# Block 2's recurrence: outputs as full 128x128 products, state products on column halves, outer products on row halves

## The chip, the cores and the metric

The kernel runs on one core of a Trainium2 chip. The metric is the device time of one execution in microseconds (us). The profile shows one execution of the program, taken on that core by the hardware profiler. TensorE (PE) does the matmuls, VectorE (DVE) and ScalarE (ACT) the elementwise work and the copies out of PSUM, GpSimd (POOL) a few subtractions, and SyncE (SP) issues most weight loads from HBM. In the profile's matmul rows `64*128` is the part of the 128x128 array that the instruction uses (rows*columns), and `64x128` its moving operand.

## What is computed

Two transformer blocks follow each other on 256 tokens of width 1024. The first has band attention, a gated delta rule and a retrieval of experts. The second has a gated linear recurrence (HGRN2), stick-breaking attention, an output projection and a feed-forward part. The change lies in the recurrence of the second block, which works on chunks of 64 tokens with a state of 128x128 for each of 8 heads:

```python
def step(state, inp):
    q_c, k_c, v_c, g_c = inp
    cum = jnp.cumsum(g_c, axis=-2)
    ...
    scores = jnp.einsum('bhtd,bhtsd,bhsd->bhts', q_c, decay, k_c)
    o = (jnp.einsum('bhts,bhsv->bhtv', scores, v_c)
         + jnp.einsum('bhtd,bhdv->bhtv', q_c * jnp.exp(cum), state))
    last = cum[:, :, -1:, :]
    state = (jnp.exp(last[:, :, 0, :, None]) * state
             + jnp.einsum('bhsd,bhsv->bhdv', k_c * jnp.exp(last - cum), v_c))
    return state, o
```

So each chunk's output is the sum of a product within the chunk (scores by values) and a product with the state before the chunk. 256 tokens are four chunks, c = 0 to 3; the first chunk has no state before it, and the state after the last is not needed.

## The kernel before

Weights stream through a feeder: each unit is a 128x1024 tile of float32 weights (`raw`), split by ACT into a rounded part (`whi`) and by DVE into the rest (`wlo`). Each such matmul is done as three products in float32r (function `mm3`): activations high by weights high, high by low, low by high. In the trace these are the rows `acc<-whi,hT_hi`, `acc<-wlo,hT_hi`, `acc<-whi,hT_lo` and their like; they are called fill below. They run whenever the chains of dependent work have nothing ready, and in block 2 they come in a fixed order of units: the recurrence's inputs first, then the attention's q, k and v, then the gates, then the output projections and the feed-forward part.

`stage_b` drives four chains beside the fill: `hgrn_chain` twice (group 0 and 1 of four heads each), `hg_out_chain` (gates and transposes the recurrence's output) and `stick_chain` (the stick-breaking attention, which starts when its values `sv` have been made). A planner (`Clock`, `drive`) writes the order of the program, and a scheduler with its own timeline then sets the final order of each engine. Engines work through their queues in that order. PSUM has two pools: `tp` with two banks, `acc` with six.

`hgrn_chain` first makes the decayed scores `sT` in six levels (tiles `hg_Z`, products `tp<-hg_Z`, and a DVE copy under a mask for each half of 128 tokens). `sT[:, i, h]` is a 128x128 tile for two chunks; its blocks between the two chunks stay zero. Tile `b_f` holds in one buffer both `sT` and the queries `q`, so that both kinds of output product read `b_f` in the trace. `b_hi` is the values `v`, `hg_kT` the transposed decayed keys, `hg_S` the states. What the change touches is the end of the function:

- Lines 1744 to 1761: for c = 0, 1, 2 the outer products of keys and values (`tp<-b_hi,hg_kT`, 64 tokens of contraction, the upper or lower row half of the array), four heads one after another, then the state of that chunk: an ACT copy for c = 0, else four DVE operations `hg_S<-hg_S,hg_el,tp`.
- Lines 1764 to 1776: for each half i of 128 tokens one PSUM bank takes the outputs of two chunks. For each head and chunk there is a product within the chunk (`acc<-b_hi,b_f`, 64 rows by 64 columns of the array), and, but for c = 0, the product with the state (`acc<-hg_S,b_f`, all 128 rows by 64 columns) accumulated on it. Then ACT squares the bank (`hg_sq`), ACT copies it (`oh<-acc`), and DVE sums the squares (`hg_ss`) for the norm.

All of it is float32 and each such product leaves two records in the trace.

Of the kernel before, what the change touches and what calls it, by code (L numbers as in the profile page):

```python
# [10 lines left out]
F32 = mybir.dt.float32  # L11
# [6 lines left out]
AF = mybir.ActivationFunctionType  # L18
ALU = mybir.AluOpType
# [70 lines left out]
def rsqrt(g, pool, ss, n, mult, out=None, eps=EPS):  # L90

    nc = g.nc
    g.n_rsqrt += 1
    tile = lambda name, dt=F32: pool.tile([128, n], dt, name=f"rs{g.n_rsqrt}_{name}")
    v, yi, t = tile("v"), tile("i", I32), tile("t")
    y = out if out is not None else tile("y")
    nc.vector.tensor_scalar(v, ss, mult, eps, op0=ALU.mult, op1=ALU.add)
    nc.vector.tensor_scalar(yi, v.bitcast(I32), 1, None, op0=ALU.logical_shift_right)
    nc.vector.tensor_scalar(yi, yi, -1.0, float(0x5F3759DF), op0=ALU.mult, op1=ALU.add)
    nc.vector.tensor_scalar(v, v, -0.5, None, op0=ALU.mult)  # L100
    cur = yi.bitcast(F32)
    for _ in range(3):
        nc.vector.tensor_tensor(t, cur, cur, op=ALU.mult)
        nc.vector.tensor_tensor(t, t, v, op=ALU.mult)
        nc.vector.scalar_tensor_tensor(y, t, 1.5, cur, op0=ALU.add, op1=ALU.mult)
        cur = y
    return y
# [155 lines left out]
def mm(g, out, lhsT, rhs, start=True, stop=True, **kw):  # L263


    ins = g.nc.tensor.matmul(out, lhsT=lhsT, rhs=rhs, start=start, stop=stop, **kw)
    g.tc.stamp_issue_order_token(ins.ins, g.tokens.get(out.tensor.name, out.tensor.name))


def transpose(g, out, src, ident=None):  # L270
    g.nc.tensor.transpose(out, src, g.c["ident"] if ident is None else ident)
# [198 lines left out]
def in_order(g, token, tile):  # L470

    g.tokens[tile.tensor.name if hasattr(tile, "tensor") else tile.name] = token
    return tile
# [312 lines left out]
def transposes4(g, src, name="tp"):  # L786

    ps = g.ps_t.tile([128, 4, 128], F32, name=name)
    for h in range(4):
        transpose(g, ps[:, h], src(h))  # L790
    return ps
# [888 lines left out]
def hgrn_chain(g, pool, st, grp):  # L1680

    nc = g.nc
    H4, I2 = range(4), range(2)
    tile4 = lambda name, **k: pool.tile([128, 4, 128], F32, name=name, **k)
    tok = lambda i: slice(i * 128, (i + 1) * 128)
# [12 lines left out]
    for h in H4:  # L1698
# [4 lines left out]
                                 op0=ALU.mult, op1=ALU.add)  # L1703
    yield 0
    yield from need(g, st.have, f"q{grp}")
    q = st.have[f"q{grp}"]
    sT = x.rearrange("p h t -> p (h t)").rearrange("p (i h t) -> p i h t", i=2, h=4)
    for i in I2:
        ps = g.ps_t.tile([128, 4, 128], F32, name="tp")
# [4 lines left out]
    for lv, b in enumerate((32, 16, 8, 4, 2, 1)):  # L1714
# [4 lines left out]
        for c in range(2):  # L1719
            nc.gpsimd.tensor_tensor(z2[:, :, c], c2[:, :, c], c2[:, :, 0, b - 1:b].to_broadcast([128, nb, b]),  # L1720
                                    op=ALU.subtract)
# [3 lines left out]
        for i in I2:  # L1725
            ps = g.ps_t.tile([128, 4, 128], F32, name="tp")
            for h in H4:
# [4 lines left out]
    el = pool.tile([128, 4, 4], F32, name="hg_el", bufs=2)  # L1732
    nc.scalar.activation(el.rearrange("p h n -> p (h n)"), c16[:, :, 63], AF.Exp)
    kd = Z()
    nc.gpsimd.tensor_tensor(kd.rearrange("p h (n t) -> p (h n) t", t=64), c16, c16[:, :, 63:64].to_broadcast([128, 16, 64]),
                            op=ALU.subtract)
# [4 lines left out]
    yield from need(g, st.have, f"hi{grp}")  # L1741
    v = st.have[f"hi{grp}"]
    Sx = [None]
    for c in range(3):
        i, r = c // 2, slice((c % 2) * 64, (c % 2) * 64 + 64)
        if c % 2 == 0:
            kT = tile4("hg_kT", bufs=2)
            nc.scalar.activation(kT, transposes4(g, lambda h: kd[:, h, tok(i)]), AF.Copy)
            yield 0
        ps = g.ps_t.tile([128, 4, 128], F32, name="tp")  # L1750
        for h in H4:
            mm(g, ps[:, h], lhsT=kT[r, h], rhs=v[r, i, h * 128:(h + 1) * 128])
        s = tile4(f"hg_S{grp}{c}")
        if c == 0:
            nc.scalar.activation(s, ps, AF.Copy)
        else:
            for h in H4:
                nc.vector.scalar_tensor_tensor(s[:, h], Sx[-1][:, h], el[:, h, c:c + 1], ps[:, h],
                                               op0=ALU.mult, op1=ALU.add)
        Sx.append(s)  # L1760
        yield 0
    ss = pool.tile([128, 2, 4], F32, name="hg_ss", bufs=2)
    oi = lambda i: st.oh[:, i, grp * 512:grp * 512 + 512].rearrange("p (h d) -> p h d", h=4)
    for i in I2:
        ps = g.ps_acc.tile([128, 4, 128], F32, name="acc")
        for h in H4:
            for c in (2 * i, 2 * i + 1):
                r = slice((c % 2) * 64, (c % 2) * 64 + 64)
                mm(g, ps[r, h], lhsT=sT[r, i, h, r], rhs=v[r, i, h * 128:(h + 1) * 128], start=True, stop=c == 0)
                if c:  # L1770
                    mm(g, ps[r, h], lhsT=q[:, h, c * 64:c * 64 + 64], rhs=Sx[c][:, h], start=False, stop=True)
        sq = tile4("hg_sq", tag="hg_kT", bufs=2)
        nc.scalar.activation(sq, ps, AF.Square)
        nc.scalar.activation(oi(i), ps, AF.Copy)
        nc.vector.tensor_reduce(ss[:, i], sq, axis=AX.X, op=ALU.add)
        yield 0
    r = rsqrt(g, pool, ss.rearrange("p i h -> p (i h)"), 8, 1.0 / 128).rearrange("p (i h) -> p i h", i=2)
# [414 lines left out]
```

## Time and profile before

| what | value |
|---|---|
| median of 3 runs | 1671.07 us (1669.23 to 1672.56) |
| profiled execution | 1672.44 us |
| its span in the trace | 1670.7 us |
| PE busy | 1613.2 us, 97% of the span |
| DVE busy | 1095.7 us, 66% |
| ACT busy | 843.9 us, 51% |
| mean granted clock of TensorE | 0.989 |

The span is the time from the first to the last instruction of the profiled execution, 1.7 us less than that execution's own time. Busy times overlap. A matmul's record runs from its start to its modelled end and overlaps the next one; what a product costs in a row of products is therefore read from start to start.

### The profile page before, as it was taken

How to read it: one execution, taken by the hardware profiler on the slowest of the kernel's cores; microseconds unless marked ns; L12 is line 12 of the kernel's file. 1: busy time of each engine (PE TensorE's matmuls, PEld its weight loads, DVE VectorE, ACT ScalarE, POOL GpSimd, SP SyncE). 2: the span in 40 equal slices, each digit the busy share in tenths (PEclk: the TensorE clock that was granted, in tenths of full speed). 3: DMA queues.
4: the chain of work that ended last, by engine and by line, in shares of the span. 5: the costliest groups of instructions: out<-in, count | busy, mean ns of one | idle time of the engine just before them, and what ended most of it. 6: DMA issues, size and time to landing. Idle time of an engine off the chain costs nothing.

```text
span 1670.7 us, 28861 instructions
## 1 busy us (share of the span) xinstructions
PE 1613.2 (97%) x11368; PEld 1427.7 (85%) x11368; DVE 1095.7 (66%) x2030; ACT 843.9 (51%) x1314; POOL 335.9 (20%) x277
## 2 busy tenths in 40 slices
PE   7999979998999999999999999999999999999998
PEld 4878757888999999998888888799777898889997
DVE  3874766899867777874444444489785554665555
ACT  4553545654554444445545545455543776554443
POOL 0000001254422223232222222123321201000000
PEclk9999989999999999999999999999999999999999
DMA  8763335454555555556666666653443443456664
GB/s 328 251 219 98 127 121 185 140 164 152 167 164 165 165 169 160 165 175 191 194 195 191 193 196 191 196 155 114 127 125 89 140 151 119 154 156 187 183 186 139
DMA packets 77897, 279.38 MB, mean 167 GB/s; under 512 B 9664, under 2 KB 10048, under 8 KB 77632
## 3 DMA queue, kind: packets, MB, share of 16 engines
q1 hardware_dynamic: 71136, 257.72, 50.1%
q10 hardware_dynamic: 6624, 19.80, 3.6%
q8 instruction: 89, 1.46, 0.4%
q14 instruction: 48, 0.39, 0.1%
HBM read 276.44 MB, written 1.05 MB: 166 GB/s over the span
## 4 chain that ended last, share of the span: by engine, by line
PE 74%; DVE 8%; ACT 1%; issue 1%; POOL 1%; DVEq 0%; ACTq 0%
PE acc L237 69%; PE tp L237 5%; DVE wlo L237 2%; DVE q_v L237 1%; DVE q_i L237 1%; DVE b_f L237 1%; DVE hg_Z L237 1%; ACT whi L237 0%; DVE q_oh L237 0%; POOL wlo L237 0%; POOL hg_Z L237 0%; DVE q_sc L237 0%; DVE b_k L237 0%; ACT hg_Z L237 0%; DVE q_pos L237 0%
## 5 line engine op out<-in xcount | busy, mean ns | idle before, releaser
L237 DVE TENSOR_TENSOR wlo<-raw,whi 128x1024 fp32r<-128x1024 f32 x415 | 517.0, 1247 | 377.6 <-ACT whi L237 376.7
L237 ACT ACTIVATE whi<-raw 128x1024 fp32r<-128x1024 f32 x470 | 495.2, 1055 | 409.6 <-PE acc L237 322.8
L237 PE MATMUL acc<-hT_hi,wlo 128*128 128x256 f32 x1728 | 491.5, 285 | 9.5 <-DVE wlo L237 7.7
L237 PE MATMUL acc<-hT_hi,whi 128*128 128x256 f32 x1728 | 493.1, 286 | 2.1 <-ACT whi L237 1.6
L237 PE MATMUL acc<-hT_lo,whi 128*128 128x256 f32 x1728 | 491.7, 285 | 1.0 <-DVE hT_lo L237 0.8
L237 PEld LDWEIGHTS acc<-hT_hi,wlo 128*128 128x128 f32 x1728 | 332.1, 192 | 13.5 <-DVE wlo L237 10.0
L237 PEld LDWEIGHTS acc<-hT_hi,whi 128*128 128x128 f32 x1728 | 331.6, 192 | 6.0 <-ACT whi L237 2.0
L237 PEld LDWEIGHTS acc<-hT_lo,whi 128*128 128x128 f32 x1728 | 332.3, 192 | 3.1 <-DVE hT_lo L237 1.4
L237 PE MATMUL acc<-wlo,hT_hi 128*128 128x512 f32 x832 | 328.4, 395 | 2.0 <-DVE wlo L237 2.0
L237 PE MATMUL acc<-whi,hT_lo 128*128 128x512 f32 x832 | 324.6, 392 | 0.0
L237 PE MATMUL acc<-whi,hT_hi 128*128 128x512 f32 x832 | 262.3, 395 | 0.9 <-ACT hT_hi L237 0.9
L237 POOL TENSOR_TENSOR wlo<-raw,whi 128x1024 fp32r<-128x1024 f32 x55 | 142.2, 2585 | 394.8 <-ACT whi L237 349.9
L237 PEld LDWEIGHTS acc<-wlo,hT_hi 128*128 128x128 f32 x832 | 156.8, 188 | 36.8 <-DVE wlo L237 2.5
L237 PEld LDWEIGHTS acc<-whi,hT_hi 128*128 128x128 f32 x832 | 156.4, 189 | 35.9 <-issue 3.2
L237 PEld LDWEIGHTS acc<-whi,hT_lo 128*128 128x128 f32 x832 | 156.8, 189 | 33.0 <-issue 0.8
L237 POOL TENSOR_TENSOR hT_lo<-A,hT_hi 128x256 fp32r<-128x256 f32 x128 | 97.1, 761 | 241.6 <-ACT hT_hi L237 241.6
L237 ACT ACTIVATE hT_hi<-A 128x256 fp32r<-128x256 f32 x128 | 52.8, 417 | 159.8 <-PE acc L237 159.8
L237 DVE TENSOR_TENSOR oh<-oh1e,c_g 128x512 f16<-128x512 f16 x128 | 75.0, 626 | 10.2 <-PE tp L237 9.5
L237 POOL TENSOR_TENSOR hg_Z<-b_k 128x512 f32<-128x512 f32 (+1 forms) x26 | 40.7, 1590 | 97.4 <-DVE b_k L237 41.4
L237 DVE SCALAR_TENSOR_TENSOR A<-tp,A 128x512 f32<-128x512 f32 (+26 forms) x52 | 28.4, 546 | 27.9 <-PE tp L237 27.8
L237 DVE TENSOR_TENSOR oh1e<-c_ih,iota 128x512 f16<-128x512 f16 x64 | 43.7, 683 | 0.9
L237 POOL TENSOR_TENSOR sb_nr<-sb_n,sb_nr 128x512 fp32r<-128x512 f32 x12 | 18.3, 1529 | 123.9 <-ACT sb_nr L237 123.9
(397 smaller groups left out, 1832.8 us busy)
## 6 DMA issues: line engine op xcount, KB each, us to landing
raw<-in_down SPq DMA_DIRECT2D x128, 512.0 KB, 3.7
raw<-in_up SPq DMA_DIRECT2D x128, 512.0 KB, 4.2
raw<-in_w_in SPq DMA_DIRECT2D x100, 512.0 KB, 3.7
raw<-in_w_ffn_in SPq DMA_DIRECT2D x44, 512.0 KB, 4.2
ada_raw<-in_w_ada ACTq DMA_DIRECT2D x32, 512.0 KB, 4.6
raw<-in_w_ffn_out SPq DMA_DIRECT2D x22, 512.0 KB, 4.3
ada_q<-in_w_ada SPq DMA_DIRECT2D x16, 512.0 KB, 6.4
raw<-in_w_query SPq DMA_DIRECT2D x16, 512.0 KB, 3.6
```

Of the source, the lines that this page charges most:

```text
L237: r = f(*args, **kw)
```

## The change

The outer products of chunks 0 and 1 go into two PSUM banks that are open together, and their instructions alternate, head by head, between the upper and the lower row half of the array. For the outputs, the products within the chunks become one 128x128x128 product per head and half (both chunks at once, the zero blocks of `sT` included) into a bank `ps`. The products with the states go into a second bank `pq`, for the second half alternating between the column halves of the array (chunk 2 writes partitions 0 to 63, chunk 3 partitions 64 to 127). ACT copies `ps` to `oh`, DVE adds `pq` to it (64 partitions for the first half, 128 for the second), and ACT squares `oh` from SBUF.

```diff
--- before.py
+++ after.py
@@ -1741,37 +1741,44 @@
     yield from need(g, st.have, f"hi{grp}")
     v = st.have[f"hi{grp}"]
     Sx = [None]
-    for c in range(3):
-        i, r = c // 2, slice((c % 2) * 64, (c % 2) * 64 + 64)
-        if c % 2 == 0:
-            kT = tile4("hg_kT", bufs=2)
-            nc.scalar.activation(kT, transposes4(g, lambda h: kd[:, h, tok(i)]), AF.Copy)
+    row = lambda c: slice((c % 2) * 64, (c % 2) * 64 + 64)
+    for cs in ((0, 1), (2,)):
+        i = cs[0] // 2
+        kT = tile4("hg_kT", bufs=2)
+        nc.scalar.activation(kT, transposes4(g, lambda h: kd[:, h, tok(i)]), AF.Copy)
+        yield 0
+
+        kv = {c: in_order(g, f"hg_kv{grp}{i}", g.ps_t.tile([128, 4, 128], F32, name="tp")) for c in cs}
+        for h in H4:
+            for c in cs:
+                mm(g, kv[c][:, h], lhsT=kT[row(c), h], rhs=v[row(c), i, h * 128:(h + 1) * 128])
+        for c in cs:
+            s = tile4(f"hg_S{grp}{c}")
+            if c == 0:
+                nc.scalar.activation(s, kv[c], AF.Copy)
+            else:
+                for h in H4:
+                    nc.vector.scalar_tensor_tensor(s[:, h], Sx[-1][:, h], el[:, h, c:c + 1], kv[c][:, h],
+                                                   op0=ALU.mult, op1=ALU.add)
+            Sx.append(s)
             yield 0
-        ps = g.ps_t.tile([128, 4, 128], F32, name="tp")
-        for h in H4:
-            mm(g, ps[:, h], lhsT=kT[r, h], rhs=v[r, i, h * 128:(h + 1) * 128])
-        s = tile4(f"hg_S{grp}{c}")
-        if c == 0:
-            nc.scalar.activation(s, ps, AF.Copy)
-        else:
-            for h in H4:
-                nc.vector.scalar_tensor_tensor(s[:, h], Sx[-1][:, h], el[:, h, c:c + 1], ps[:, h],
-                                               op0=ALU.mult, op1=ALU.add)
-        Sx.append(s)
-        yield 0
     ss = pool.tile([128, 2, 4], F32, name="hg_ss", bufs=2)
     oi = lambda i: st.oh[:, i, grp * 512:grp * 512 + 512].rearrange("p (h d) -> p h d", h=4)
     for i in I2:
-        ps = g.ps_acc.tile([128, 4, 128], F32, name="acc")
+
+
+        ps, pq = (in_order(g, f"hg_o{grp}{i}", g.ps_acc.tile([128, 4, 128], F32, name="acc")) for _ in range(2))
         for h in H4:
-            for c in (2 * i, 2 * i + 1):
-                r = slice((c % 2) * 64, (c % 2) * 64 + 64)
-                mm(g, ps[r, h], lhsT=sT[r, i, h, r], rhs=v[r, i, h * 128:(h + 1) * 128], start=True, stop=c == 0)
-                if c:
-                    mm(g, ps[r, h], lhsT=q[:, h, c * 64:c * 64 + 64], rhs=Sx[c][:, h], start=False, stop=True)
+            mm(g, ps[:, h], lhsT=sT[:, i, h], rhs=v[:, i, h * 128:(h + 1) * 128])
+        cs = (2 * i, 2 * i + 1) if i else (1,)
+        for h in H4:
+            for c in cs:
+                mm(g, pq[row(c), h], lhsT=q[:, h, c * 64:c * 64 + 64], rhs=Sx[c][:, h])
+        rs = slice(0 if i else 64, 128)
+        nc.scalar.activation(oi(i), ps, AF.Copy)
+        nc.vector.tensor_tensor(oi(i)[rs], oi(i)[rs], pq[rs], op=ALU.add)
         sq = tile4("hg_sq", tag="hg_kT", bufs=2)
-        nc.scalar.activation(sq, ps, AF.Square)
-        nc.scalar.activation(oi(i), ps, AF.Copy)
+        nc.scalar.activation(sq, oi(i), AF.Square)
         nc.vector.tensor_reduce(ss[:, i], sq, axis=AX.X, op=ALU.add)
         yield 0
     r = rsqrt(g, pool, ss.rearrange("p i h -> p (i h)"), 8, 1.0 / 128).rearrange("p (i h) -> p i h", i=2)
```

The helper `in_order` names a token of issue order for the products of these banks, as elsewhere in the kernel.

On PE, at the outer products of group 0, the program of before has the four products of chunk 0 into one bank (`tp_12655`) and then the four of chunk 1 into another (`tp_12704`):

```order
L237 MATMUL acc_12640<-whi_12668,hT_hi_11710 128x512
L237 MATMUL tp_12655<-b_hi0_12171,hg_kT_12624 128x128 x4
L237 MATMUL tp_12704<-b_hi0_12171,hg_kT_12624 128x128 x4
L237 MATMUL acc_12640<-wlo_12669,hT_hi_11710 128x512
L237 MATMUL acc_12640<-whi_12668,hT_lo_11711 128x512
```

In the changed program the same eight products alternate between the two banks:

```order
L237 MATMUL acc_12640<-whi_12673,hT_hi_11710 128x512
L237 MATMUL tp_12655<-b_hi0_12171,hg_kT_12624 128x128
L237 MATMUL tp_12656<-b_hi0_12171,hg_kT_12624 128x128
L237 MATMUL tp_12655<-b_hi0_12171,hg_kT_12624 128x128
L237 MATMUL tp_12656<-b_hi0_12171,hg_kT_12624 128x128
L237 MATMUL tp_12655<-b_hi0_12171,hg_kT_12624 128x128
L237 MATMUL tp_12656<-b_hi0_12171,hg_kT_12624 128x128
L237 MATMUL tp_12655<-b_hi0_12171,hg_kT_12624 128x128
L237 MATMUL tp_12656<-b_hi0_12171,hg_kT_12624 128x128
L237 MATMUL acc_12640<-wlo_12674,hT_hi_11710 128x512
```

The number and size of these products are the same; their order differs, and the fill around them stays where it was.

On PE, at the second half of group 0's outputs, the program of before alternates products with the states after chunks 1 and 2 (`hg_S01`, `hg_S02`) and products within the chunks (`b_hi0`), all into one bank; two of the `tp<-hg_Z` rows of group 1's levels stand between:

```order
L237 MATMUL acc_13005<-whi_12909,hT_lo_11711 128x512
L237 MATMUL acc_12863<-hg_S02_12777,b_f0_11907 64x128
L237 MATMUL acc_12863<-b_hi0_12171,b_f0_11907 64x128
L237 MATMUL tp_12788<-hg_Z_12726 128x128 x4
L237 MATMUL tp_12844<-hg_Z_12794 128x128 x4
L237 MATMUL acc_12863<-hg_S01_12709,b_f0_11907 64x128
L237 MATMUL acc_12863<-b_hi0_12171,b_f0_11907 64x128
L237 MATMUL acc_12863<-hg_S02_12777,b_f0_11907 64x128
L237 MATMUL acc_12863<-b_hi0_12171,b_f0_11907 64x128
L237 MATMUL acc_12863<-hg_S01_12709,b_f0_11907 64x128
```

The changed program has only the products with the states here, into the bank `acc_12868`, two neighbours on different column halves; the products within the chunks stand some 65 rows earlier, as one row `acc_12867<-b_hi0_12171,b_f0_11907 128x128 x4`:

```order
L237 MATMUL acc_12768<-whi_12830,hT_hi_11710 128x512
L237 MATMUL acc_12868<-hg_S02_12777,b_f0_11907 64x128
L237 MATMUL acc_12868<-hg_S01_12703,b_f0_11907 64x128
L237 MATMUL acc_12868<-hg_S02_12777,b_f0_11907 64x128
L237 MATMUL tp_12788<-hg_Z_12723 128x128 x4
L237 MATMUL tp_12848<-hg_Z_12794 128x128 x4
L237 MATMUL acc_12868<-hg_S01_12703,b_f0_11907 64x128
L237 MATMUL acc_12868<-hg_S02_12777,b_f0_11907 64x128
L237 MATMUL acc_12868<-hg_S01_12703,b_f0_11907 64x128
L237 MATMUL acc_12868<-hg_S02_12777,b_f0_11907 64x128
L237 MATMUL acc_12768<-wlo_12831,hT_hi_11710 128x512
```

What were 13 products, each of another shape than its neighbours, are here seven products of one shape in two pieces, of three and four.

On DVE, at the same place, the program of before goes on from the copies under a mask to the next level's product and the sum of squares:

```order
L237 SCALAR_TENSOR_TENSOR hg_S02_12777<-hg_S01_12709,hg_el_12598,tp_12772 128x128 x4
L237 COPY_PREDICATED b_f1_12334<-hgm_11864,tp_12782 128x512
L237 TENSOR_TENSOR wlo_12999<-raw_12836,whi_12998 128x1024
L237 TENSOR_TENSOR wlo_13019<-raw_12913,whi_13018 128x1024
L237 COPY_PREDICATED b_f1_12334<-hgm_11864,tp_12788 128x512
L237 COPY_PREDICATED b_f1_12334<-hgm_11864,tp_12844 128x512
L237 TENSOR_TENSOR hg_Z_13042<-hg_Z_13042,b_k1_12417 128x512
L237 TENSOR_REDUCE hg_ss_12801<-hg_sq_12880 128x4
L237 TENSOR_SCALAR rs12_v_12937<-hg_ss_12801 128x8
L237 TENSOR_TENSOR hg_Z_13042<-hg_Z_13042,b_f1_12334 128x512
```

In the changed program the addition of the second bank stands between, ahead of the next level's product `hg_Z_13071`, and the sum of squares comes later:

```order
L237 SCALAR_TENSOR_TENSOR hg_S02_12777<-hg_S01_12703,hg_el_12598,tp_12772 128x128 x4
L237 COPY_PREDICATED b_f1_12334<-hgm_11864,tp_12782 128x512
L237 TENSOR_TENSOR wlo_12983<-raw_12834,whi_12982 128x1024
L237 COPY_PREDICATED b_f1_12334<-hgm_11864,tp_12788 128x512
L237 COPY_PREDICATED b_f1_12334<-hgm_11864,tp_12848 128x512
L237 TENSOR_TENSOR oh_11709<-oh_11709,acc_12868 128x512
L237 TENSOR_TENSOR hg_Z_13071<-hg_Z_13071,b_k1_12417 128x512
L237 TENSOR_TENSOR wlo_13003<-raw_12909,whi_13002 128x1024
L237 TENSOR_REDUCE hg_ss_12801<-hg_sq_12883 128x4
L237 TENSOR_TENSOR hg_Z_13071<-hg_Z_13071,b_f1_12334 128x512
```

The addition is queued behind the masked copies of group 1 and waits for the last product into `acc_12868`; the sum of squares has moved behind one split of weights.

## Rows read from the trace of the kernel before

**Rows 1.** The page, part 1 (busy us) and part 4 (chain that ended last).

```profile
PE 1613.2 (97%) x11368; PEld 1427.7 (85%) x11368; DVE 1095.7 (66%) x2030; ACT 843.9 (51%) x1314; POOL 335.9 (20%) x277
...
PE 74%; DVE 8%; ACT 1%; issue 1%; POOL 1%; DVEq 0%; ACTq 0%
```

**Rows 2.** Busy us by stretch: PE, PEld, DVE, ACT, POOL, then clock, DMA share, GB/s.

```profile
1190.00:1290.00 100.00, 96.99 (x532) 73.51 (x531) 72.01 (x152) 45.33 (x58) 20.60 (x15) 1.00 0.35 104
...
1230.00:1250.00 20.00, 20.00 (x110) 17.19 (x109) 19.97 (x44) 11.83 (x14) 2.34 (x2) 1.00 0.41 120
```

**Rows 3.** Groups of PE by shape, 1040 to 1420 us: records, busy us, mean ns.

```profile
L237 PE MATMUL acc<-hg_S,b_f 128*64 128x128 f32 x48 | 10.4, 298 | 0.0
L237 PE MATMUL acc<-b_hi,b_f 64*64 64x128 f32 x64 | 10.3, 294 | 0.0
...
L237 PE MATMUL tp<-b_hi,hg_kT 64*128 64x128 f32 x48 | 7.3, 297 | 0.3 <-ACT hg_kT L237 0.3
```

**Rows 4.** Timeline of PE, group 0's outputs: start, us, instruction, records.

```profile
1196.26 1.95 PE L237 MATMUL tp<-hg_Z 128*128 128x128 f32 x16
1198.14 0.43 PE L237 MATMUL acc<-hg_S,b_f 128*64 128x128 f32 x2
1198.50 0.44 PE L237 MATMUL acc<-b_hi,b_f 64*64 64x128 f32 x4
1198.87 0.43 PE L237 MATMUL acc<-hg_S,b_f 128*64 128x128 f32 x2
...
1201.77 0.50 PE L237 MATMUL acc<-wlo,hT_hi 128*128 128x512 f32 x1
1202.10 0.39 PE L237 MATMUL acc<-whi,hT_lo 128*128 128x512 f32 x1
1202.33 0.40 PE L237 MATMUL acc<-whi,hT_hi 128*128 128x512 f32 x1
```

**Rows 5.** Timeline of PE, group 0's outer products of chunks 0 and 1.

```profile
1190.18 0.39 PE L237 MATMUL acc<-whi,hT_hi 128*128 128x512 f32 x1
1190.50 1.71 PE L237 MATMUL tp<-b_hi,hg_kT 64*128 64x128 f32 x16
1192.14 0.50 PE L237 MATMUL acc<-wlo,hT_hi 128*128 128x512 f32 x1
```

**Rows 6.** Timeline of PE before and at group 1's outer products; waits in brackets.

```profile
1252.74 1.16 PE L237 MATMUL tp<-hg_Z 128*128 128x128 f32 x8 [1.84 <-DVE rs_t L237]
1254.74 0.63 PE L237 MATMUL tp<-consts,hg_Z 128*128 128x128 f32 x4 [0.84 <-DVE b_f L237]
...
1256.06 1.71 PE L237 MATMUL tp<-b_hi,hg_kT 64*128 64x128 f32 x16 [0.32 <-ACT hg_kT L237]
1257.69 0.43 PE L237 MATMUL acc<-b_hi,b_f 64*64 64x128 f32 x2
```

**Rows 7.** Timeline of PE, group 1's outer products of chunk 2 between transposes.

```profile
1270.48 0.48 PE L237 MATMUL tp<-b_hi,hg_kT 64*128 64x128 f32 x2
1270.90 0.33 PE L237 MATMUL tp<-consts,b_sq 128*128 128x128 f32 x1
1271.16 0.49 PE L237 MATMUL tp<-b_hi,hg_kT 64*128 64x128 f32 x2
```

**Rows 8.** Timeline of PE, stick-breaking values: eight products on one column half.

```profile
1329.76 0.43 PE L237 MATMUL tp<-sb_w,b_sv 128*64 128x128 f32 x2
...
1331.34 0.38 PE L237 MATMUL tp<-sb_a,b_sv 128*64 128x128 f32 x2
1331.65 0.39 PE L237 MATMUL acc<-hT_lo,whi 128*128 128x256 f32 x1
```

**Rows 9.** Timeline of PE, block 1: eight products on four column strips of 32.

```profile
203.00 1.07 PE L237 MATMUL acc<-ada_raw,sc 128*32 128x256 f32 x16
204.00 0.44 PE L237 MATMUL tp<-consts,at_s 128*128 128x128 f32 x2
```

**Rows 10.** Instructions on the output tile: ns min/median/max, first and last start.

```profile
L237 DVE TENSOR_TENSOR oh<-oh,rs_y x4: 679/683/692, 1235.2 to 1290.0; 128x512 f32<-128x512 f32 x4
L237 POOL TENSOR_TENSOR oh<-oh,b_hg x4: 1287/1559/1861, 1311.9 to 1329.1; 128x512 f32<-128x512 f32 x4
```

## The prediction

> **What bounds the kernel now.** I read the page's busy times first. PE is busy for 97% of the span, and the chain of work that ended last runs through PE for 74% and through DVE for 8% [rows 1]. So time is mostly what PE's instructions occupy, and the rest is places where another engine's chain sets the pace. The busy times by stretch narrow this to the recurrence: between 1190 and 1290 us PE is busy for 97.0 of 100 us, while DVE has 28 us and ACT 55 us to spare; but from 1230 to 1250 DVE is full (19.97 of 20) [rows 2]. PE's only waits in these 100 us are just behind that full stretch, 1.84, 0.84 and 0.32 us [rows 6]. So a product that PE no longer pays for should shorten the span by its own time, except where DVE is full.
>
> The groups by shape count the work: 24 state products (48 records, two each), 32 products within chunks (64 records) and 24 outer products (48) [rows 3]. Then I read the timeline of PE, from start to start, for what each costs.
>
> **Prices from the timeline.** Eight products on the full array take from 1196.26 to 1198.14, 1.88 us, of which the last carries some 0.09 us for the change of shape behind it: 0.224 us each [rows 4]. From 1198.14 to 1201.77 stand ten stretches that alternate between the 128*64 and the 64*64 part of the array, 3.63 us, 0.363 each. A stretch of two 64*64 products (four records) takes 0.37 us (1198.50 to 1198.87), a single 128*64 product 0.36 (1198.14 to 1198.50) [rows 4]: two products on opposite quarters go side by side for free, and each stretch pays for a change of shape. How much: eight products on one column half, without a change between, take 1.89 us [rows 8]. With p for a product and e for the change, 8p + e = 1.89 and p + e = 0.363, so p = 0.218 and e = 0.145.
>
> On row halves a single product with a full-array product behind it takes 0.42 us (1270.48 to 1270.90) [rows 7], so with 0.224 for the product the change is worth 0.19. The full-array work on both sides also pays: the fill product ahead of the outer products holds PE for 0.32 us [rows 5] and the one behind the outputs for 0.33, where its neighbour takes 0.23 [rows 4]. That is 0.09 and 0.10, so 0.2 us for each visit to a part of the array, besides e.
>
> **The change part by part.**
>
> *Outputs removed.* The timeline of before has 48 such stretches in the two groups (24 of state products, 24 of products within chunks, of which eight are pairs); the ten above are part of them. 48 x 0.363 = 17.4 us.
>
> *Products within chunks added.* 2 groups x 2 halves x 4 heads = 16 full products, no change of shape to their neighbours: 16 x 0.224 = 3.6 us.
>
> *State products.* All 24 remain. By the order of the changed program they stand in ten stretches, of 4, 1, 3 and 4 in group 0 and 4, 1, 2, 1, 1 and 3 in group 1. In the stretches of four for the first half there is one chunk, one column half, and no partner. In the others neighbours alternate between halves, and five pairs form. The trace of before has no such pair. From below, a pair costs as much as one product, from above as two. The nearest row has four column strips of 32: 16 records of 256 columns in 1.00 us [rows 9]. A record of 128 columns takes half of 0.224, so one of 256 some 0.22, and one after another they would take 3.6 us (my estimate from rows 4): all four strips ran together. I take a pair as one product: 24 - 5 = 19 x 0.218 = 4.1 us, and ten changes at 0.145, 1.5 us: 5.6 us.
>
> The Trainium skill, page "TensorE: Matmul & The Clock Gate", in its part 3 on packing small matmuls, says that a weight load overlaps matmuls in flight only where the row group differs. By that rule column halves, which share all rows, would not run side by side, and the sum at the end would be 1.1 us smaller. [rows 9] speak against it, since those strips share all rows too.
>
> *Outer products.* For chunks 0 and 1 they now take 1.64 us, in both groups (1190.50 to 1192.14 and 1256.06 to 1257.69) [rows 5, 6]. Eight one after another would be 8 x 0.224 + 0.19 = 1.98, so 0.34 us overlaps already, where chunk 0's last products meet chunk 1's first. Alternating, I expect four pairs: 4 x 0.224 + 0.19 = 1.09, which saves 0.55 in each group, 1.1 together. From above: no overlap at all, 1.98, a loss of 0.34 each. I take the lower end, since the overlap on the same row halves is there already [rows 5]. For chunk 2 group 0 keeps its four singles between other products; group 1's four now stand together, 4 x 0.224 + 0.19 = 1.09 for 4 x 0.415 = 1.66: 0.6 saved.
>
> *Visits.* These products left the full shape 22 times before and do so 17 times in the changed order: 5 x 0.2 = 1.0 saved. But the scheduler also splits the attention's first scores (64 rows) into more stretches, 16 for 13: 3 x (0.19 + 0.2) = 1.2 lost.
>
> Sum on PE: -17.4 + 3.6 + 5.6 - 1.1 - 0.6 - 1.0 + 1.2 = -9.7 us.
>
> *DVE and ACT.* Four additions are new on DVE, each of 512 columns as `oh<-oh,rs_y`, 0.68 us [rows 10]: 2.7 us. ACT does the same two operations per half. The chain behind an output gets longer by an addition and a hand-over, but its result is last scaled at 1290 and first used by POOL at 1311.9 [rows 10], some 20 us of cover. Without it each half would cost about 1 us more. On DVE itself 28 us are free in the 100 [rows 2], so two of the additions, and those of group 1 after 1257, are hidden. Group 0's second one falls just ahead of the full stretch, and the order puts one more split of weights before the last masked copy that PE waits for: some 2 us more for DVE there. In the same place PE has 129 fill products to do where it had 106, 23 x 0.23 = 5.3 us, less the 3.6 saved at the outputs of group 0's second half (13 x 0.363 less 4 x 0.218 and 2 x 0.145): 1.7 us more. So the waits of 1.84 and 0.84 us [rows 6] should about stay. The third, 0.32, is for the transposed keys (ACT), and the order now has 18 fill products between; it should go, but a wait of that size may come elsewhere. I count zero.
>
> *Behind an addition that waits.* DVE's addition waits for the last state product and ACT's copy; behind it stand group 1's next level products. PE does the state products directly behind the `tp<-hg_Z` rows whose masked copies DVE has ahead of the addition, and a pair of masked copies outlasts them. So nothing is held up.
>
> *PSUM.* Each half holds two of the six `acc` banks instead of one. Fill needs two, and two for the group that is being copied out, so all six are used while a half is open. No wait for a bank stands in the trace of before; I take zero, and a late copy as a rival.
>
> The profiled span is 1670.7 us and becomes 1661.0. The profiled execution (1672.44) lies 1.4 us above the median of the runs shown, so the median goes from 1671.07 to **1661.4 us**.
>
> **Rivals.**
>
> *The halves don't run side by side.* Then the outer products lose 2 x 0.89 and the state pairs 1.1: -6.8 us, 1664.3. The overlaps in [rows 5, 9] speak against it. If row halves do and column halves don't, only the 1.1 us of the state pairs is lost: 1662.5; the four strips [rows 9] speak against that. The Trainium skill's rule above gives this last case.
>
> *DVE takes its place.* If DVE's full stretch sets the end of group 1's levels alone, PE gets there earlier and waits longer: the saving of group 0 (half of 9.7, less the fill that is there to do) is waited away, 3 to 5 us, 1664.5 to 1666.5. For it: DVE full, and PE's waits behind it. Against it: the planner has put 23 more fill products there.
>
> *The waits vanish.* The extra fill covers all three, 3.0 us: 1658.4.
>
> *Banks: slower.* A fill group that begins while both banks of a half are open must wait until ACT has copied the group before it and DVE has added. Nine groups begin in the 100 us (48 fill products of 0.23 us each, 11 us). The price is what the copies are late: to lose 9.7 and 3.3 more, each would have to wait 1.4 us. The trace shows PE waiting for no such copy today, with one bank fewer to spare. 1675 us or more.
>
> *Nothing changes.* Only if all the saving is covered by waits for other engines, as for a chain that sets the end by itself; the chain is PE's for 74%. 1671.
>
> **Chances.** The forecast as summed, within 2 us: 61%. No halves side by side: 5%. Row halves alone: 4%. DVE takes its place: 14%. Waits vanish: 9%. Nothing: 4%. Slower: 3%. Measurement tells a change from none at about 0.2%, 3.3 us, so faster is below 1667.7. All but the last two are faster, with a little lost to waits larger than I see: 0.91, same 0.05, slower 0.04. The range takes in vanished waits below (1658.4, less 1 us for the median's scatter) and DVE's upper end above: 1657.5 to 1666.5.
>
> **What the next profile would show.** Right: outer products of chunks 0 and 1 in about 1.1 us; within-chunk rows as 128*128 at 0.22 us each; state products in ten stretches, 5.6 us with their changes; PE's busy time some 9 to 10 us lower. Wrong, if the stretches are as expected and the span is not: then PE's waits between 1200 and 1290 grew, for DVE's `b_f`, for `wlo`, or for a copy out of `acc`. If the pairs take 0.44 us, the halves don't overlap.

## The result, and the profile after

The changed kernel took 1660.54 us, the median of 4 runs (1657.71 to 1661.22), beside 1671.29 us for the kernel before (4 runs, 1669.23 to 1672.56): a ratio of 0.9926, 95% interval 0.9906 to 0.9946. The forecast was 1661.4. A later series gave 0.9924 (0.991 to 0.9937), some 12.7 us. The ratios in this document are those on record, estimated from the runs with their intervals; they are not quotients of the two medians (here that would be 0.9936). The profiled execution took 1660.82 us.

The page of the changed kernel, span, busy times and chain, to be held against [rows 1]:

```profile
span 1658.8 us, 28802 instructions
...
PE 1604.5 (97%) x11336; PEld 1426.3 (86%) x11336; DVE 1094.6 (66%) x2034; ACT 844.4 (51%) x1314; POOL 337.3 (20%) x277
...
PE 75%; DVE 7%; ACT 1%; issue 1%; POOL 1%; DMA 0%; DVEq 0%; ACTq 0%
```

PE is busy for 8.7 us less, and the span is 11.9 us shorter. So some of the gain is idle time. The busy times by stretch, columns as in [rows 2], show where:

```profile
1190.00:1290.00 100.00, 100.00 (x558) 81.66 (x555) 79.02 (x164) 54.66 (x73) 21.28 (x15) 1.00 0.42 128
```

PE, which stood still for 3.0 of these 100 us before, is now never idle. The groups by shape from 1185 to 1440 us (records, busy us, mean ns) answer [rows 3]:

```profile
L237 PE MATMUL acc<-hg_S,b_f 128*64 128x128 f32 x48 | 6.3, 287 | 0.0
L237 PE MATMUL tp<-b_hi,hg_kT 64*128 64x128 f32 x48 | 5.4, 291 | 0.0
L237 PE MATMUL acc<-b_hi,b_f 128*128 128x128 f32 x32 | 4.2, 274 | 0.0
```

The counts are the forecast's: 24 state products, 24 outer products, and 16 full products for 32 quarter ones. The timeline of PE in group 0 gives the price of each, from start to start (before: [rows 4, 5]):

```profile
1189.03 1.16 PE L237 MATMUL tp<-b_hi,hg_kT 64*128 64x128 f32 x16
1190.12 0.50 PE L237 MATMUL acc<-wlo,hT_hi 128*128 128x512 f32 x1
...
1192.98 1.05 PE L237 MATMUL acc<-b_hi,b_f 128*128 128x128 f32 x8
1193.79 0.48 PE L237 MATMUL acc<-wlo,hT_hi 128*128 128x512 f32 x1
...
1195.98 1.09 PE L237 MATMUL acc<-hg_S,b_f 128*64 128x128 f32 x8
1196.99 0.50 PE L237 MATMUL acc<-whi,hT_lo 128*128 128x512 f32 x1
...
1218.26 0.66 PE L237 MATMUL acc<-hg_S,b_f 128*64 128x128 f32 x8
1218.85 0.50 PE L237 MATMUL acc<-wlo,hT_hi 128*128 128x512 f32 x1
```

The eight outer products of chunks 0 and 1 take 1.09 us for 1.64. Four state products on one column half take 1.01 (1195.98 to 1196.99); four that alternate between the halves take 0.59 (1218.26 to 1218.85). Summed over both groups the state products take 5.61 us in ten stretches, the full products 3.49.

One more reading is needed before times are compared: the granted clock. First before, then after, around the recurrence:

```profile
1180.00:1190.00 10.00, 7.97 (x31) 6.11 (x30) 6.88 (x8) 4.30 (x6) 0.00 (x0) 0.83 0.49 156
...
1450.00:1500.00 50.00, 46.61 (x276) 40.53 (x275) 32.58 (x56) 26.01 (x40) 0.00 (x0) 1.00 0.52 159
```

```profile
1180.00:1190.00 10.00, 7.98 (x48) 6.17 (x47) 7.04 (x8) 4.46 (x6) 0.00 (x0) 1.00 0.48 156
...
1450.00:1500.00 50.00, 46.61 (x297) 42.46 (x296) 31.02 (x56) 24.75 (x40) 0.00 (x0) 0.93 0.50 151
```

In both stretches PE is busy equally long in both kernels (8.0 of 10 and 46.6 of 50 us), on code that the change does not touch. Part of one execution's stretch ran at the lower level (1.2 GHz), and not the other's. That gave the changed execution 1.5 us ahead of the recurrence (its first outer product starts at 1189.03 for 1190.50) and cost it 2.8 us behind it: from the first product of the attention's output projection to the end, the same records take 252.8 us before and 255.6 after. That product starts here, first before, then after:

```profile
1417.86 0.38 PE L237 MATMUL acc<-b_sbT_hi,whi 128*128 128x256 f32 x1
```

```profile
1403.20 0.38 PE L237 MATMUL acc<-b_sbT_hi,whi 128*128 128x256 f32 x1
```

Between the first outer product and this one both executions have a clock of 1.00 and the same fill. There before takes 227.4 us and the changed kernel 214.2: 13.2 us less. Single executions of one kernel differ by as much as the clock made here (1668.66 to 1677.97 us over 17 runs of before in one later series).

### The profile page after: what moved, and what is told of

Read it like the earlier page. It is cut to its first block, busy times and chain, and to the rows that moved or that the text cites. A ratio compares the mean times of both kernels' runs of the same rounds, so it can differ in the third digit from the quotient of the medians.

```text
span 1658.8 us, 28802 instructions
## 1 busy us (share of the span) xinstructions
PE 1604.5 (97%) x11336; PEld 1426.3 (86%) x11336; DVE 1094.6 (66%) x2034; ACT 844.4 (51%) x1314; POOL 337.3 (20%) x277
## 3 DMA queue, kind: packets, MB, share of 16 engines
HBM read 276.44 MB, written 1.05 MB: 167 GB/s over the span
## 4 chain that ended last, share of the span: by engine, by line
PE 75%; DVE 7%; ACT 1%; issue 1%; POOL 1%; DMA 0%; DVEq 0%; ACTq 0%
PE acc L237 70%; PE tp L237 5%; DVE wlo L237 2%; DVE hg_Z L237 1%; DVE b_f L237 1%; DVE q_v L237 1%; DVE q_i L237 1%; DVE q_oh L237 0%; POOL wlo L237 0%; ACT whi L237 0%; POOL hg_Z L237 0%; DVE b_k L237 0%; DVE q_sc L237 0%; DVE xt L237 0%; ACT hg_Z L237 0%
```

## The experiments

Ratios are to the kernel before on the same chip, with 95% intervals. "Waits" are those of PE between 1190 and 1290 us; before has 3.0 us. Its state products take 8.70 us.

| version | ratio | waits, us | state products, us |
|---|---|---|---|
| changed, again | 0.9924 (0.991 to 0.9937) | 0 | 5.61 |
| outputs alone | 0.9951 (0.9933 to 0.997) | 0.9 | 5.25 |
| outer products alone | 0.9996 (0.9983 to 1.0009) | 2.9 | 8.35 |
| changed, by chunk | 0.9938 (0.9921 to 0.9955) | 0 | 6.69 |
| changed, one bank | 0.9941 (0.992 to 0.9961) | 2.6 | 4.73 |
| changed, more DVE work | 0.9911 (0.9896 to 0.9927) | 0 | 5.10 |
| before, other order | 0.9979 (0.9966 to 0.9993) | 0 | 8.35 |
| changed, attention in pairs | 0.9843 (0.9829 to 0.9856) | 0 | 5.61 |
| one bank, attention in pairs | 0.9854 (0.9834 to 0.9874) | 2.6 | 4.74 |

### The two halves of the change apart

"Outputs alone" puts the old loop of the outer products (c by c, the `-` lines up to `Sx.append(s)` of the change's diff) back into the changed kernel. "Outer products alone" puts the old output loop back.

> The new outputs (full products, states' products in a second bank) with the old outer products, one chunk after the other. My theory (the change is worth what its products occupy on TensorE, start to start): outputs removed -17.4, 16 full products +3.6, the states' products in nine stretches with ten pairs fewer than singles would need +5.2, chunk 0's four outer products of one group left as singles +1.1, chunk 2's of that group together -0.6, visits and the attention's first scores +1.2: -6.9 us, a ratio of 0.9959 (0.994 to 0.998), TensorE busy some 7 us less. Rival, the waits decide (the changed kernel's three vanished waits belong to its order): the same sum, and another 3 us only if the three waits behind the full VectorE stretch are gone here too, 0.994. Rival, the gain is the outer products' and not the outputs': 0.998 to 1.0.

> The old outputs with the new outer products, chunks 0 and 1 alternating between row halves. My theory: 0.55 us in each group, 1.1, and two visits fewer, 0.4: -1.5 us, a ratio of 0.9991 (0.998 to 1.001), each run of 16 records in 1.09 us where it was 1.64, and the outputs' 48 stretches at 0.363 us as before. Rival, halves share the work only by the old accident of a late start: 1.6 to 2.0 us for the 16 records, ratio 1.000 to 1.001. Rival, the three waits of before (1.84, 0.84, 0.32 us) shrink by the order alone: ratio 0.997.

The outputs alone give 8.2 us by the ratio (5.0 to 11.2), for a sum of 6.9 and waits of 0.9 us where 3.0 stood: 9.0. Its wait is another one, for transposes of the attention; the three of before are gone. The outer products alone give nothing that can be measured, and 1.5 was expected. Their timeline of PE, in group 0 and then in group 1:

```profile
1190.31 1.16 PE L237 MATMUL tp<-b_hi,hg_kT 64*128 64x128 f32 x16
1191.40 0.50 PE L237 MATMUL acc<-wlo,hT_hi 128*128 128x512 f32 x1
...
1255.09 1.62 PE L237 MATMUL tp<-b_hi,hg_kT 64*128 64x128 f32 x16 [0.32 <-ACT hg_kT L237]
1256.64 0.43 PE L237 MATMUL acc<-b_hi,b_f 64*64 64x128 f32 x2
```

Group 0 has the expected 1.09 us. In group 1 the same 16 records take 1.55 us: the records of the second row half begin only 0.47 us after those of the first. The timelines of PE's weight loads and of DVE show what they wait for:

```profile
1255.08 0.29 PEld L237 LDWEIGHTS tp<-b_hi,hg_kT 64*128 64x128 f32 x2 [0.56 <-ACT hg_kT L237]
1255.55 0.96 PEld L237 LDWEIGHTS tp<-b_hi,hg_kT 64*128 64x128 f32 x14 [0.17 <-DVE rs_y L237]
```

```profile
1254.78 0.71 DVE L237 COPY_PREDICATED b_f<-hgm,tp 128x512 f32<-128x512 int32 x1
```

DVE's last masked copy reads a `tp` bank until 1255.50, and the loads for the second bank start 0.05 us later, as the first ones do after ACT's copy (1255.03). The view names the small operation next to the copy. There are two `tp` banks, and the alternating products need both. In the changed kernel fill stands ahead of these products and the last masked copy ends 3.6 us before they start; they take 1.09 us in both groups. So alternating pays in full only where both banks are free when the run begins.

### By chunk instead of alternating

```diff
-        for h in H4:
-            for c in cs:
+        for c in cs:
+            for h in H4:
                 mm(g, pq[row(c), h], lhsT=q[:, h, c * 64:c * 64 + 64], rhs=Sx[c][:, h])
```

> As the changed kernel, but a half's states' products go chunk by chunk, not alternating between column halves. My theory (neighbours on opposite column halves run side by side): pairs are lost, runs of four on one half take 4 x 0.218 + 0.145 = 1.02 us; the states' products take 6.7 us for 5.6, the gain of the changed kernel is 1.1 to 1.3 us smaller, ratio 0.9935 to 0.996, which the trace tells and the times hardly. Rival, the halves overlap by themselves in any order: 5.6 us again and the changed kernel's ratio. Rival, column halves never share time and the 0.587 us for eight records comes from something else: 5.6 us again.

Its timeline of PE, four state products of group 0's second half, all of chunk 2:

```profile
1199.73 1.09 PE L237 MATMUL acc<-hg_S,b_f 128*64 128x128 f32 x8
1200.75 0.50 PE L237 MATMUL acc<-wlo,hT_hi 128*128 128x512 f32 x1
```

Eight records on one half take 1.02 us, the eight alternating ones 0.59, and the ten stretches 6.69 us for 5.61. The theory holds: column halves share time when neighbours are on opposite halves, and only then. The times (0.9938 for 0.9924) lean the same way, within their intervals.

### The second bank and the additions

"One bank" lets the state products accumulate onto the full products and drops the addition:

```diff
-            mm(g, ps[:, h], lhsT=sT[:, i, h], rhs=v[:, i, h * 128:(h + 1) * 128])
+            mm(g, ps[:, h], ..., start=h == 0, stop=True, skip_group_check=True)
...
-                mm(g, pq[row(c), h], lhsT=q[:, h, c * 64:c * 64 + 64], rhs=Sx[c][:, h])
+                mm(g, ps[row(c), h], ..., start=False, stop=True, skip_group_check=True)
```

"More DVE work" goes the other way, behind each addition of the changed kernel:

```diff
+        for _ in range(4):
+            nc.vector.tensor_tensor(oi(i), oi(i), oi(i), op=ALU.max)
```

> As the changed kernel, but the states' products accumulate onto the full products in the same bank: no second bank, no addition on VectorE, ScalarE's two operations as in the kernel before. Seven stretches of states' products for ten. My theory (second bank and addition are hidden): TensorE's sum -10.2 us against before, ratio 0.993 (0.991 to 0.995), the same as the changed kernel within 0.5 us; any wait for the group of products to finish shows in ScalarE alone. Rival, the additions or the banks cost on the path: 1.5 to 3 us faster than the changed kernel, ratio 0.991 or less. Rival, accumulating column halves onto a full product makes TensorE wait for its own writes: states' products dearer than 0.22 us each, ratio 0.995 or more.

> As the changed kernel, with four more VectorE operations of 128x512 (a maximum of a tile with itself, no change of its values) directly behind each of the four additions: 16 x 0.68 = 10.9 us more of VectorE work, and each half's chain some 2.8 us longer. My theory (additions and their chain are hidden, VectorE has 20 us to spare in these 100): no more than 0.5 us from the chain; the ten operations that fall ahead of VectorE's full stretch use up its 5.4 us of idle time, so up to 2 us of waits may come back behind the masked copies: 0 to +2.5 us against the changed kernel, ratio to before 0.992 to 0.9955. Rival (VectorE sets the pace in group 1's levels, and the additions are on it): two thirds or more of 10.9 us come through, ratio 0.997 or more.

> The changed kernel once more, beside the others of this series, for a ratio with more runs and a second trace. From the first trace: outputs, states' and outer products as there to 0.01 us (ten stretches, 5.61 us; 16 records of outer products in 1.09 us), no wait of TensorE between 1190 and 1290 us, ratio 0.9915 to 0.9945. If the vanished waits were luck of one execution, waits of 0.8 us and more stand there now.

The 16 added operations are there, at 0.69 us in the median, DVE is busy for 87.57 us in the 100, and PE still never waits in them. First the stretch, then the instructions on the output tile (ns min/median/max, first and last start), of this version:

```profile
1190.00:1290.00 100.00, 100.00 (x562) 81.70 (x561) 87.57 (x176) 52.13 (x65) 21.16 (x15) 1.00 0.42 126
```

```profile
L237 DVE TENSOR_TENSOR oh<-oh x16: 672/688/1166, 1201.7 to 1282.0; 128x512 f32<-128x512 f32 x16
```

So the additions and their chain are hidden, and DVE's load does not set the pace in this order. One bank is no faster than two, though nothing is lost on the products themselves: three alternating take 0.58 us and four 0.59 in both versions, so accumulating onto the full products costs PE nothing. It has less work on PE and DVE, but waits again, which was not expected, in its timeline of PE:

```profile
1245.42 1.95 PE L237 MATMUL tp<-hg_Z 128*128 128x128 f32 x16
1248.85 1.16 PE L237 MATMUL tp<-hg_Z 128*128 128x128 f32 x8 [1.48 <-DVE b_f L237]
1251.08 1.09 PE L237 MATMUL tp<-consts,hg_Z 128*128 128x128 f32 x4 [1.07 <-DVE rs_y L237]
```

These rows follow each other: as in before, no fill stands between them. By stretch, this execution paid a second time:

```profile
1246.00:1250.00 4.00, 2.52 (x21) 2.14 (x19) 3.97 (x14) 2.22 (x3) 2.04 (x2) 1.00 0.71 230
1250.00:1258.00 8.00, 6.93 (x25) 6.04 (x25) 6.50 (x22) 0.60 (x1) 3.14 (x4) 0.57 0.22 67
```

PE was idle for 1.5 of 4 us, and then had a mean granted clock of 0.57 for 8 us, mostly the lower level. The kernel before waits as long in the same place at a clock of 1.00, so it does not follow every such wait.

### Where the waits come from

The forecast kept before's three waits, and they vanished. The timelines of DVE and of POOL, both of before, show what stands just ahead of the first of them [rows 6]:

```profile
1249.60 1.04 DVE L237 SCALAR_TENSOR_TENSOR rs_y<-rs_t,rs_i 128x16 f32<-128x16 f32 x1
1250.67 0.96 DVE L237 TENSOR_TENSOR rs_t<-rs_y 128x16 f32<-128x16 f32 x1
...
1251.97 0.72 DVE L237 COPY_PREDICATED b_f<-hgm,tp 128x512 f32<-128x512 int32 x1
...
1253.88 0.72 DVE L237 COPY_PREDICATED b_f<-hgm,tp 128x512 f32<-128x512 int32 x1
```

```profile
1249.56 2.04 POOL L237 TENSOR_TENSOR b_sq<-b_sq,rs_y 128x512 f32<-128x512 f32 x2 [14.31 <-DVE rs_t L237]
```

Operations of 128x16 take 0.16 to 0.19 us elsewhere in this stretch, but for two beside POOL's next pair. These two end with POOL's two multiplications of the attention's queries, which GpSimd does beside its subtractions. The test leaves POOL's work out: a first try took the pair of the first query tile, which runs earlier, the second one multiplication of the right pair.

```diff
-            for i in range(2):
+            for i in range(2 if (m, n) != (0, 1) else 1):
                 nc.gpsimd.tensor_tensor(x[:, i], x[:, i], bc(r[:, i], 2, 64), op=ALU.mult)
```

> The kernel before, with GpSimd's two multiplications of the attention's first query tile left out (the queries of the first eight heads stay unscaled; nothing else is left out, and VectorE has the same operations in the same order up to TensorE's waits). In the trace of before these two run from 1249.56 to 1251.60 us, and in that time VectorE has two operations of 128x16 that take 1.04 and 0.96 us instead of 0.17, directly ahead of the masked copy on which TensorE waits 1.84 us. My theory: GpSimd holds VectorE up, and the wait of 1.84 us falls to 0.3 us or less, with both small operations at 0.17 us. Rival (VectorE is full by its own work, or the order of fill alone makes the wait): the small operations or what follows fill the time, and 1.5 us or more of the wait stay.

> The kernel before, with one of GpSimd's two multiplications of the attention's second query tile left out (128 tokens of the queries of heads 8 to 15 stay unscaled). The run before this one left out the pair of the first tile, which runs earlier; the pair that stands in VectorE's way is the second tile's. On TensorE and VectorE the order in group 1's levels is that of before: 26 fill products ahead of the last but one level, none between it and the outer products. Theory (GpSimd holds VectorE up): one of the two small operations of VectorE ahead of the masked copy is back at 0.17 us for 0.96, and TensorE's wait of 1.84 us becomes 1.0 to 1.1 us. Rival (the order of fill alone, VectorE has other work to fill the time): the wait stays at 1.7 us or more.

> The kernel before, with GpSimd's two multiplications of that second query tile cut to one head of eight each (the queries of heads 9 to 15 stay unscaled). With them this short the scheduler puts group 1's last levels as in the changed kernel: 27, 19 and 19 fill products where the kernel before has 26 and then none. Theory (the changed kernel's vanished waits are worth what they were, apart from the products): no wait of TensorE between 1190 and 1290 us, 3.0 us less, ratio 0.998 (0.9965 to 0.9995). Rival (the waits only move, because VectorE is what is full): 2 us or more of waits for VectorE's masked copies or splits elsewhere, ratio 0.9995 to 1.001.

The first try changed nothing in that place: POOL's pair at 1251.19, small operations of 1.03 and 0.97 us, waits of 2.9 us in all; it was aimed at the wrong pair. With one multiplication left out, in the timelines of DVE and PE:

```profile
1245.29 1.03 DVE L237 SCALAR_TENSOR_TENSOR rs_y<-rs_t,rs_i 128x16 f32<-128x16 f32 x1
1246.36 0.17 DVE L237 TENSOR_TENSOR rs_t<-rs_y 128x16 f32<-128x16 f32 x1
```

```profile
1247.64 1.16 PE L237 MATMUL tp<-hg_Z 128*128 128x128 f32 x8 [1.05 <-DVE rs_t L237]
1249.56 0.63 PE L237 MATMUL tp<-consts,hg_Z 128*128 128x128 f32 x4 [0.76 <-DVE rs_t L237]
```

The second operation is back at 0.17 us and the wait is 1.05 for 1.84: 0.79 us, as the theory said. So one multiplication makes 0.8 us of this wait; that both make most of the 1.84 is an estimate from it, since both at once were not left out in the same order. (That single execution took 1670.25 us; one run says nothing on the time.)

In the changed kernel the same hold-up is there, and PE does not see it. Its timelines of DVE and then of PE (the rows between the two of PE are fill, 19 products):

```profile
1246.61 1.01 DVE L237 TENSOR_TENSOR rs_t<-rs_y 128x16 f32<-128x16 f32 x1
1247.55 0.75 DVE L237 COPY_PREDICATED b_f<-hgm,tp 128x512 f32<-128x512 int32 x1
```

```profile
1243.02 1.95 PE L237 MATMUL tp<-hg_Z 128*128 128x128 f32 x16
...
1249.15 1.05 PE L237 MATMUL tp<-hg_Z 128*128 128x128 f32 x8
```

In before the same 16 records stand directly ahead of the first row of [rows 6], without a fill product between these two rows or between the next ones:

```profile
1248.95 1.95 PE L237 MATMUL tp<-hg_Z 128*128 128x128 f32 x16
```

"Other order" is the kernel before with POOL's pair cut to one head of eight; the scheduler then places 27 fill products ahead of these 16 records and 19 and 20 behind them, and no wait is left in the 100 us. It gains 2.1e-3 (0.7 to 3.4), 3.5 us where 3.0 was expected. So the waits do not move elsewhere. From the first outer product to the output projection, with the same fill, it is 4.0 us shorter than before: 3.0 of waits, the rest in products beside them and in the order, which also put group 1's outer products side by side (1.09 us for 1.64).

This run changes POOL's work and the order together. The other versions tell them apart: the waits come with the order. The changed kernel has the hold-up, and its second masked copy of this level ends 5.3 us after the 16 records began, for 5.6 before; the 19 fill products cover that. "Outputs alone" has its last masked copies about as late as before (60.9, 62.8 and 67.4 us after the first outer product, for 61.5, 63.4 and 65.2) and 24 fill products between: none of the three waits. One bank has them earlier (56.2, 58.3 and 60.2) and no fill between: waits of 1.5 and 1.1 us. In all thirteen traces these waits stand where no fill lies between the two rows (six versions), and in none of the seven with fill there. POOL's work sets part of the length of a wait that nothing covers.

### The same lever on the attention

The stick-breaking attention takes four tiles of two heads at a time, and of each first the one head and then, a bank later, the other (r = 0, 1), each on one half of the array. Here both go together, and one bank takes the values of both (shortened; the edit also reorders the attention's steps and moves some buffers):

```diff
-    banks = [(p0, r, *kq) for p0 in (0, 4) for r in range(2) for kq in ((1, 1), (0, 1), (0, 0))]
+    banks = [(p0, *kq) for p0 in (0, 4) for kq in ((1, 1), (0, 1), (0, 0))]
...
         for j in range(4):
-            mm(g, z[:, j], lhsT=kT[pr, p0 + j, ...], rhs=qT[pr, p0 + j, ...], ...)
+            for r in R2:
+                mm(g, z[r][:, j], lhsT=kT[pr(r), p0 + j, ...], rhs=qT[pr(r), p0 + j, ...], ...)
...
-        split_to(g, sbT.hi[ix], sbT.lo[ix], ps[pr])
+        split_to(g, sbT.hi[ix], sbT.lo[ix], ps)
```

> The changed kernel, with the same lever used on the stick-breaking attention: the two heads of a tile (row halves of the array for the scores, column halves for the values) are worked on together, product by product alternating, the values of both into one bank with one copy out for two. Today 96 records of scores take 13.8 us and 96 of values 13.1 us, one half at a time. My theory: side by side, six times 16 records of scores in 1.09 us and some split ones, 7.5 us; values 6.4 us; some 14 fewer changes of shape at 0.2 us for their full neighbours: 13 to 15 us less than the changed kernel, ratio to before 0.983 to 0.986. Rival (the attention's chain of ScalarE, VectorE and GpSimd, now six rounds of two heads, sets the end): TensorE waits ahead of the output projection, less than half of it comes through, ratio 0.989 or more. Rival (no overlap): as the changed kernel, 0.992.

> The attention in pairs, as in the run before, on the version of the outputs with one bank and no addition. That version has three stretches of states' products fewer than the changed kernel (0.9 us) but 2.6 us of waits in group 1's levels, by its order, which this edit should leave as it is. Theory: 1 to 3 us slower than the pairs on the changed kernel, ratio to before 0.985 to 0.987, with the waits of 1.5 and 1.1 us still there. Rival (the waits go with the order of the attention's first products): 0.983 to 0.9845, the fastest of all.

The pairs on the changed kernel take 1647.68 us (5 runs, 1644.61 to 1649.79) beside 1674.54, 0.9843: the fastest version, 14.0 us below the changed kernel in the same series (1661.67). Its timeline of PE, scores and then values (only values stand between the last two lines):

```profile
1313.26 1.16 PE L237 MATMUL acc<-b_qT,b_kT 64*128 64x128 f32 x16
1314.35 0.38 PE L237 MATMUL acc<-hT_hi,whi 128*128 128x256 f32 x1
...
1329.23 0.44 PE L237 MATMUL tp<-sb_w,b_sv 128*64 128x128 f32 x4
...
1331.12 0.39 PE L237 MATMUL acc<-hT_hi,whi 128*128 128x256 f32 x1
```

Sixteen records of scores, of both halves, take the 1.09 us that eight of one half took. The 32 records of values take 1.89 us (1329.23 to 1331.12), as the 16 of one half did [rows 8]. By the trace all scores are 5.8 us cheaper and all values 5.5, and no wait of PE is left from 1190 to 1440 us; how much of the rest is the new order of steps was not tried. With one bank the waits of 1.5 and 1.1 us are back, as expected, and the version is slower by about their size, within the intervals.

## Why the prediction was right, and where it was not

**The sum held, term by term.** From start to start: the outputs removed, 17.4 us as forecast; full products 3.49 (3.6); state products 5.61 (5.6); outer products of chunks 0 and 1 -1.10 (-1.1), of chunk 2 -0.58 (-0.6); the attention's first scores +0.58 and full-array neighbours some -0.3, together +0.3 where visits and scores were put at +0.2. That is some -9.6 us for -9.7. "Outputs alone", "by chunk" and the timelines bear out each of the large ones; the pairs on column halves, the one price with no row of before, was taken from the right neighbour [rows 9].

**Column halves.** By the Trainium skill, page "TensorE: Matmul & The Clock Gate", part 3, a weight load overlaps matmuls in flight only where the row group differs. The prediction took from this that column halves would not share time; 0.59 us for the alternating four and 1.02 for the others say that here they do. That part of the Trainium skill's page doesn't say so either: its table of measured speedups has 2.38 times for three column tiles, its figure and not this case's.

**The step that failed: "I count zero" for PE's waits.** It rested on masked copies that would come some 2 us later while PE got there 1.7 us later. They came earlier: counted from the first outer product, the last three began at 61.5, 63.4 and 65.2 us before and 55.5, 58.5 and 62.4 after. DVE, which the prediction took for full, had idle time ahead of its full stretch, some of it for PE's outputs. Before, the sum of squares waited for them:

```profile
1225.95 0.69 DVE L237 TENSOR_REDUCE hg_ss<-hg_sq 128x4 f32<-128x512 f32 x1 [2.37 <-ACT hg_sq L237]
```

After, no such wait stands there. DVE's idle time from the first outer product to the last masked copy fell from 10.8 to 7.8 us. But early copies were not what removed the waits, as "one bank" and "outputs alone" show. The prediction counted the fill up to these places (129 products for 106) and not where in it the last levels stand: before has none behind the 16 records, the changed order 19 and 19. So the rival "the waits vanish", at 9%, came on top of the sum: -9.6 - 3.0 = -12.6 us, against 12.7 in the second series. "DVE takes its place" falls with "more DVE work": in an order with fill between the levels, 10.9 us of it cost nothing.

**Why the time was still right.** The stretch of equal fill is 13.2 us shorter: 9.6 of products, 3.0 of waits, and some 0.6 that stand mostly in the products next to the waits (the two `tp<-hg_Z` rows around the first wait take, without the waits, 1.95 and 1.16 us before and 1.70 and 0.81 after). The profiled span adds the clock: -13.2 - 1.5 + 2.8 = -11.9, as measured. By the ratios the change is worth 12.4 us in the first series and 12.7 in the second, some 3 us more than the forecast; that the first median came within 0.9 us of 1661.4 is luck, the scatter of 4 runs whose medians lie 10.75 us apart. The range held since it had room for vanished waits.

**Banks.** No wait for a copy out of `acc` appeared in these 100 us.

## What to carry to other kernels

Small products that use half of the array should alternate with partners on the other half, product by product: the pair costs what one did, and the change of shape is paid once, if the banks of both are free when the run begins. Look for every such loop; here the attention's was worth as much as the whole change. A wait that sits behind another engine's full stretch should be priced from what that engine does in those microseconds, and from how much fill the order has there, before it is called fixed.

## What the hardware showed unexpectedly

Small VectorE operations lasted until GpSimd's had ended: operations of 128x16 took 0.96 to 1.04 us for 0.17, and one was back at 0.17 when one GpSimd multiplication was left out. The Trainium skill, page "SBUF — State Buffer", section "Who interferes with whom", says that the two share a port pair under an exclusive lock, which the first to start holds for its whole instruction; this case agrees. It can go the other way too: in the changed kernel GpSimd's same pair took 4.12 us for 2.04, beside VectorE's splits of weights.
